# Two seven-product units of a decoder layer: the second unit's first weight sum, its row-sum fetches and the gate fetches are issued at other places

## The chip, the cores and the metric

The kernel is one program on one NeuronCore of a Trainium2 chip. TensorE (PE in the profile) multiplies, VectorE (DVE), ScalarE (ACT) and GpSimd (POOL) do the element-wise work, SyncE (SP) and GpSimd issue the DMAs that matter here. The metric is the device time of one execution in microseconds; lower is better. Three executions of the kernel before gave 883.59, 883.69 and 885.77 us, median 883.69.

## The reference, cut to what matters

One decoder layer on 512 tokens of width 1024, float32: a LayerNorm, then a token mixer in which gated linear attention (GLA, 4 heads) and latent attention run on the same input, then a squared-ReLU MLP. The part that concerns this change is the input projection of GLA's value `v_g` and gate `r_g`, both 512x1024 by 1024x1024, and what is done with them:

```python
q_g, k_g, v_g, r_g, a_lr, q_lat, kv_lat, gate_logits = jnp.split(h @ w_in, offsets, axis=-1)
o_gla = gla_chunked(split_heads(q_g) * GLA_HK ** -0.5, split_heads(k_g), split_heads(v_g), split_heads(log_a))
o_gla = rms_norm(o_gla.transpose(0, 2, 1, 3), gla_norm_g.reshape(GLA_HEADS, GLA_HV))
y_gla = (o_gla * jax.nn.silu(r_g)) @ w_o_gla
```

## The kernel before, in words

**Precision.** Every float32 operand is split in a high part (a rounding copy by ACT, L185 or L111) and a low part (a subtraction by DVE, L186 or L112). A product then is three matmuls: high x high, high x low, low x high. A weight item is a 128 x 1024 tile of 4 KB a partition, and its split is one ACT and one DVE instruction.

**The two units.** `unit("r")` and later `unit("v")` compute the two 512x1024 by 1024x1024 projections with seven block products in place of eight. A unit has seven phases, n = 0 to 6, each of two halves (hf = 0, 1) of 12 matmuls (L755 to L757), so 24 matmuls of 512 columns a phase. The phases multiply the weight operands `RPH = ("T1", "11", "22", "T2", "21", "T3", "T4")`. "11" and "21" are plain weight blocks, loaded by SP as `wraw` (L173). "22" is a plain block loaded by POOL as `rw`. The T's are sums of blocks that the DMA makes: `r_begin` loads a block into two `rw` tiles (T1) and then adds a second block into the same tiles with an accumulating DMA (L614); later `r_add` turns T1 into T2, T2 into T4 and "22" into T3 by further accumulating DMAs into the same tile, each of which has to wait until the split has read the former sum.

**The row sums.** The other operand of phases 0, 2, 3 and 5 is a sum of blocks of the input rows, called S1, S4, S2 and S3. They are made once while `unit("r")` is near, split, used by it and stored to DRAM (`keep`, L631). For `unit("v")` they are fetched again by POOL (`fetch`, L636): two tiles of 512 KB each.

**Order of the work.** The program is traced in one order; `tick` after each half phase advances other lanes of work (the GLA levels of each head, the SiLU of the gates, `gla_out`). A planner then orders every engine's instructions: it runs through the program with its own estimated durations and gives an engine, among the instructions whose inputs and tile slots it takes to be ready, the one that was traced first. On the chip every engine executes its list strictly in that order.

**Slots.** Tiles of 4 KB a partition (`rw`, the fetched row sums `S`, the gate and value results `rg`, the split pairs xh/xl, `qk`, `kq`, `sd` and others) share 24 slots, tag "A". Tiles of 2 KB share 22 slots, pool "B". The high and low weight tiles `whi` and `wlo` have two slots each; items take either these ("w") or a pair xh/xl from the 24 ("a"), in the order `wawawawawawaww`, so the last two items of a unit (T4) and the first of the next (T1, half 0) go through whi/wlo.

**The gates and `gla_out`.** `silus()` turns the four results of `unit("r")` into SiLU and stores them (`rd`, L728). `gla_out(h)`, one of four heads, runs after `unit("v")`. It fetches the head's gates from DRAM on SP's queue (L930, two DMAs of 256 KB into one 4 KB tile `rg`), computes four output tiles i = 0 to 3, normalises, multiplies with the gates (L971), and transposes (L978).

Of the kernel before, what the change touches and what calls it, by code (L numbers as in the profile page):

```python
# [10 lines left out]
F32 = mybir.dt.float32  # L11
# [41 lines left out]
def tile_hybrid_block(ctx: ExitStack, tc: tile.TileContext, I, out, dbg=None):  # L53
# [19 lines left out]
    def A(shape, dt=F32, n="a"):  # L73
        tag, bufs = ("C", 8) if n in TAG_C else (n, TAG_W[n]) if n in TAG_W else ("A", 24)
        return pa.tile(shape, dt, tag=tag, bufs=bufs, name=nm(n))
# [540 lines left out]
    def r_begin(sec):  # L616
        for hf in range(2):
            r_load(sec, "T1", 0, 1, hf)
        r_add(sec, "T1", "T1", 0, 0)
# [13 lines left out]
    def fetch(name):  # L633
        RS[name] = [A([P, 4, 256], F32R, name) for _ in range(2)]
        for d, w in zip(KEPT[name], RS[name]):
            nc.gpsimd.dma_start(w, d)  # L636
# [63 lines left out]
    def unit(sec, nxt=None):  # L700
        a, b = [[MM() for _ in range(2)] for _ in range(2)]
        R = {}
        val = sec == "v"

        def put(key, t, o, scale=1.0):
            if key not in R:
                R[key] = A([P, 2, T], F32, "rg")
            r = R[key][:, t]
            act(r, o, AF.Copy, scale=scale)

        def last(key, t, o, op):
            r = R[key][:, t]
            vtt(r, r, o, op=op)
            if val:
                if t == 0:
                    R["v" + key] = [A([P, 2, T], F32R, n) for n in ("vh", "vl")]
                split(r, *[w[:, t] for w in R["v" + key]])

        def silus():
            for key in ("12", "11", "22", "21"):  # L720
                for t in range(2):
                    r = R[key][:, t]
                    th = B([P, T], F32, "th")
                    act(th, r, AF.Tanh, scale=0.5)
                    stt(r, th, 1.0, r, op0=ALU.add, op1=ALU.mult)
                    yield
                d = DR([P, 2, T], F32, "rd")
                nc.sync.dma_start(d, R[key])  # L728
                R[key] = d
                yield  # L730
            Rp[0], Rp[1] = [R["11"], R["21"]], [R["12"], R["22"]]

        def lhs(n, k, t):
            c = slice(t * P, (t + 1) * P)
            d = slice(256 + t * P, 256 + (t + 1) * P)
            if n in (1, 4):
                h = hT[k + 4 * (n == 4)]
                return h[:, 0, c], h[:, 1, c]
            if n == 6:
                return hT[k + 4][:, 0, d], hT[k + 4][:, 1, d]  # L740
            key = {0: "S1", 2: "S4", 3: "S2", 5: "S3"}[n]
            while not val and key not in RS:
                step(t_rs)
            return [w[:, k, c] for w in RS[key]]

        for n in range(7):
            o = a if n in (1, 3, 5) else b
            for hf in range(2):
                pump(PL[sec, n, hf])
                for pp in range(2):  # L750
                    for t in range(2):
                        xh, xl = lhs(n, 2 * hf + pp, t)
                        hi, lo = [w[:, pp] for w in stream[PL[sec, n, hf]]["w"]]
                        opens = n in (0, 1, 4, 6) and hf == 0 and pp == 0
                        mm(o[t], xh, hi, start=opens, stop=False, skip_group_check=True)  # L755
                        mm(o[t], xh, lo, start=False, stop=False, skip_group_check=True)
                        mm(o[t], xl, hi, start=False, stop=hf == 1 and pp == 1, skip_group_check=True)  # L757
                if hf == 0 and (val or n in (0, 2, 4, 6)):
                    tick(None)
                if n == 0 and hf == 1:  # L760
                    r_add(sec, "T2", "T1", 1, 1)
                    if val:
                        fetch("S2")
                if n == 2 and hf == 1:
                    r_add(sec, "T3", "22", 0, 1)
                    if val:
                        fetch("S3")
                if n == 3 and hf == 1:
                    r_add(sec, "T4", "T2", 1, 0)
                if n == 5 and hf == 0 and nxt:  # L770
                    r_begin(nxt)
                    fetch("S1")
                    fetch("S4")
                if n == 6 and hf == 0 and nxt:
                    for h2 in range(2):
                        r_load(nxt, "22", 1, 1, h2)
            for t in range(2):
                if n == 0:
                    put("22", t, o[t], -1.0)
                elif n == 1:  # L780
                    put("11", t, o[t])
                elif n == 2:
                    put("12", t, o[t], -1.0)
                elif n == 3:
                    last("12", t, o[t], ALU.subtract)
                elif n == 4:
                    last("11", t, o[t], ALU.add)
                elif n == 5:
                    put("21", t, o[t])
                    last("22", t, o[t], ALU.subtract)  # L790
                else:
                    last("21", t, o[t], ALU.add)
            if n < 6:
                tick(None)
        if val:
            for j in range(2):
                Vp[j] = [R["v%d%d" % (i, j + 1)] for i in (1, 2)]
        else:
            t_sil.append(spawn(silus()))
# [124 lines left out]
    def gla_out(h):  # L924
        while SS[h] is None or Vp[h // 2] is None or Rp[h // 2] is None:
            yield
        sd, s128, kq = SS[h]
        rg = A([P, NT, HV], F32, "rg")
        for i in range(2):
            nc.sync.dma_start(rg[:, 2 * i:2 * i + 2], Rp[h // 2][i][:, :, h % 2 * HV:(h % 2 + 1) * HV])  # L930

        def V(j):
            c = slice(h % 2 * HV, (h % 2 + 1) * HV)
            return [t[:, j % 2, c] for t in Vp[h // 2][j // 2]]
        p = PX()[:, :HV]
        for j in range(2):
            vh, vl = V(j)
            kh, kl = [kq[:, 0, w, j * P:(j + 1) * P] for w in range(2)]
            mm(p, kh, vh, start=j == 0, stop=False)
            mm(p, kh, vl, start=False, stop=False)  # L940
            mm(p, kl, vh, start=False, stop=j == 1)
        sh, sl = B([P, HV], F32R, "gst"), B([P, HV], F32R, "gst")
        split(p, sh, sl)
        ss = S([P, NT], F32, "gss")
        ps = []
        for i in range(NT):
            if i % 2 == 0:
                ps.append(PX())
            o = ps[i // 2][:, (i % 2) * HV:(i % 2 + 1) * HV]
            todo = [(sd[:, 0, i, :], sd[:, 1, i, :], *V(i))]  # L950
            if i % 2:
                todo.append((s128[:, 0, i // 2, :], s128[:, 1, i // 2, :], *V(i - 1)))
            if i > 1:
                c = slice((i - 2) * P, (i - 1) * P)
                todo.append((kq[:, 1, 0, c], kq[:, 1, 1, c], sh, sl))
            for n, (ah, al, bh, bl) in enumerate(todo):
                mm(o, ah, bh, start=n == 0, stop=False)
                mm(o, ah, bl, start=False, stop=False)
                mm(o, al, bh, start=False, stop=n == len(todo) - 1)
            sq = B([P, HV], F32, "osq")  # L960
            act(sq, o, AF.Square, accum_out=ss[:, i:i + 1])
            if i >= 1:
                yield
        vts(ss, ss, 4.0 / HV, 4.0 * RMS_EPS, op0=ALU.mult, op1=ALU.add)
        rs = S([P, NT], F32, "grs")
        gtt(rs, ss, mhalf[:, :NT], op=ALU.pow)
        yield
        og = [B([P, 2, HV], F32, "og") for _ in range(2)]
        for i in range(NT):
            o = ps[i // 2][:, (i % 2) * HV:(i % 2 + 1) * HV]  # L970
            stt(og[i // 2][:, i % 2, :], o, rs[:, i:i + 1], rg[:, i],  # L971
                op0=ALU.mult, op1=ALU.mult)
        yield
        for kk in range(2):
            k = 2 * h + kk
            p = PX()
            for tt in range(NT):
                nc.tensor.transpose(p[:, tt * P:(tt + 1) * P], og[tt // 2][:, tt % 2, kk * P:(kk + 1) * P], ident)  # L978
            yield
            o = A([P, 2, T], F32R, "ogT")  # L980
            split(p, o[:, 0, :], o[:, 1, :], scale=glg[:, k:k + 1])
            ogT[k] = o
# [574 lines left out]
```

## Time and profile before

| | |
|---|---|
| median of three executions | 883.69 us |
| the profiled execution, device time | 883.45 us |
| its span, first to last instruction | 881.7 us |
| PE busy | 854.5 us, 97% of the span |
| DVE, ACT, POOL busy | 610.0, 466.2, 188.0 us |
| mean granted TensorE clock | 0.994 |

The profile was taken on one execution. Its times count from the first instruction, so 1.75 us of the device time lie outside the span. "Idle before" is the time an engine did nothing ahead of an instruction, with the event that ended it. `unit("r")` runs from 94.9 to 139.1 us, `unit("v")` from 145.5 to 193.0 us, and the four heads of `gla_out` from 192.8 to 307 us.

### The profile page before, as it was taken

The page shows a single profiled execution, that of the slowest core. Times are in us where ns is not written, and L with a number is a line of the kernel's source. Part 1 is how long each engine was busy: PE and PEld are TensorE (multiplying, and loading weights), DVE is VectorE, ACT ScalarE, POOL GpSimd, SP SyncE. Part 2 cuts the span into 40 slices and gives each one's busy share as a digit, 9 for nine tenths or more (in the row PEclk, how much of TensorE's full clock was granted, in tenths as well). Part 3 has the DMA queues.
Part 4 walks back from the last instruction along what each step waited for, and adds up shares of the span by engine and source line. Part 5 has one row for each costly group of instructions (what it writes and reads, how often), then busy time and mean ns, then how long its engine had stood idle before and what let it go on. Part 6 is the DMA issues. An engine that isn't in the chain of part 4 may idle for free. (4 is left out here: it accounts for less than half of the span.)

```text
span 881.7 us, 11628 instructions
## 1 busy us (share of the span) xinstructions
PE 854.5 (97%) x4288; PEld 726.2 (82%) x4288; DVE 610.0 (69%) x993; ACT 466.2 (53%) x802; POOL 188.0 (21%) x221
## 2 busy tenths in 40 slices
PE   5999997999999999999999999999999999999995
PEld 5988785778898888888988888988888888888885
DVE  7977986796556344557876797886567556754697
ACT  5467765564554433435654414565457546735662
POOL 2404683603202010000000013004400520242023
PEclk9999998999999999999999999999999999999998
DMA  7836898933454223111307527006941990398075
GB/s 229 241 103 218 250 267 227 250 124 105 122 176 120 63 63 105 52 53 55 109 25 261 191 76 282 1 1 168 291 114 30 260 256 27 68 304 202 0 191 96
DMA packets 73240, 127.35 MB, mean 144 GB/s; under 512 B 8641, under 2 KB 34676, under 8 KB 73184
## 3 DMA queue, kind: packets, MB, share of 16 engines
q1 hardware_dynamic: 50848, 70.86, 24.8%
q0 software_dynamic: 20416, 52.11, 24.7%
q10 hardware_dynamic: 1920, 3.66, 1.2%
q8 instruction: 33, 0.54, 0.2%
q14 instruction: 23, 0.19, 0.1%
HBM read 99.86 MB, written 12.58 MB: 128 GB/s over the span
## 5 line engine op out<-in xcount | busy, mean ns | idle before, releaser
L186 DVE TENSOR_TENSOR wlo<-wraw,whi 128x1024 fp32r<-128x1024 f32 (+2 forms) x90 | 102.2, 1137 | 97.8 <-ACT whi L185 92.0
L236 PE MATMUL mm<-h,whi 128*128 128x512 f32 x416 | 163.2, 393 | 0.1
L237 PE MATMUL mm<-h,whi 128*128 128x512 f32 x416 | 162.8, 391 | 0.0
L238 PE MATMUL mm<-h,wlo 128*128 128x512 f32 x416 | 155.9, 391 | 0.1
L185 ACT ACTIVATE whi<-wraw 128x1024 fp32r<-128x1024 f32 (+2 forms) x90 | 87.0, 967 | 69.9 <-PE mm L237 34.5
L1419 POOL DMA_DIRECT2D res<-ev x54 | 47.8, 992 | 237.6 <-ACT ev L1417 194.2
L236 PEld LDWEIGHTS mm<-h,whi 128*128 128x128 f32 x416 | 78.2, 188 | 16.0 <-ACT whi L185 0.3
L238 PEld LDWEIGHTS mm<-h,wlo 128*128 128x128 f32 x416 | 77.9, 188 | 16.2 <-DVE wlo L186 0.5
L237 PEld LDWEIGHTS mm<-h,whi 128*128 128x128 f32 x416 | 78.2, 188 | 15.1
L1484 ACT ACTIVATE relu<-mm 128x512 f32<-128x512 f32 x32 | 18.8, 595 | 56.9 <-PE mm L238 56.9
L374 POOL TENSOR_TENSOR mv<-mv,mhalf 128x1 f32<-128x1 f32 x4 | 4.1, 1036 | 208.5 <-DVE mv L373 208.5
L185 ACT ACTIVATE xh<-wraw 128x1024 fp32r<-128x1024 f32 (+1 forms) x24 | 23.2, 974 | 26.8 <-PE mm L271 15.4
L614 POOL DMA_DIRECT2D rw<-in_w_in_dram x24 | 26.1, 1128 | 32.6 <-DVE xl L186 12.9
L186 DVE TENSOR_TENSOR wlo<-wq,whi 128x1024 fp32r<-128x1024 f32 x15 | 18.4, 1224 | 19.9 <-ACT whi L185 19.9
L856 ACT ACTIVATE M<-qk 128x256 f32<-128x256 f32 x56 | 23.9, 454 | 14.1 <-DVE qk L838 13.3
L186 DVE TENSOR_TENSOR xl<-wraw,xh 128x1024 fp32r<-128x1024 f32 (+1 forms) x24 | 27.0, 1137 | 6.3 <-ACT xh L185 6.3
L1417 ACT ACTIVATE ev<-mm 128x512 f32<-128x512 f32 x20 | 11.9, 600 | 31.6 <-DMA res<-ev 27.8
L838 DVE TENSOR_TENSOR qk<-qk,tot 128x512 f32<-128x512 f32 x28 | 23.5, 840 | 7.1 <-PE px L894 4.2
L1334 POOL DMA_DIRECT2D wq<-in_w_ff_dram x32 | 24.5, 1024 | 11.1 <-issue 4.6
L236 PE MATMUL mm<-ogT,whi 128*128 128x512 f32 x64 | 25.7, 401 | 0.0
L237 PE MATMUL mm<-ogT,whi 128*128 128x512 f32 x64 | 25.3, 395 | 0.0
L237 PE MATMUL mm<-omT,whi 128*128 128x512 f32 x64 | 25.2, 394 | 0.0
(457 smaller groups left out, 2413.6 us busy)
## 6 DMA issues: line engine op xcount, KB each, us to landing
wraw<-in_w_in_dram SPq DMA_DIRECT2D x32, 512.0 KB, 4.6
wraw<-in_w_ff_dram SPq DMA_DIRECT2D x32, 512.0 KB, 8.6
wq<-in_w_ff_dram POOLq DMA_DIRECT2D x32, 512.0 KB, 9.9
res<-ev POOLq DMA_DIRECT2D x54, 256.0 KB, 8.6
rw<-in_w_in_dram POOLq DMA_DIRECT2D x24, 512.0 KB, 7.7
S<-s SPq DMA_DIRECT2D x8, 512.0 KB, 6.4
S<-S POOLq DMA_DIRECT2D x8, 512.0 KB, 7.1
wraw<-in_w_o_gla_dram SPq DMA_DIRECT2D x8, 512.0 KB, 3.7
```

The source lines that it names most:

```text
L185: st["ins"] = act(hi[:, :nk, :n], raw[:, :nk, :n], AF.Copy)
L186: vtt(lo[:, :nk, :n], raw[:, :nk, :n], f(hi[:, :nk, :n]), op=ALU.subtract)
L236: mm(o, hi[:, c], xh, start=first, stop=False)
L237: mm(o, hi[:, c], xl, start=False, stop=False)
L238: mm(o, lo[:, c], xh, start=False, stop=last)
L614: nc.gpsimd.dma_start(RW[sec, op, hf], w[:, k0:k0 + 2, c0:c0 + T], **({"accum_op": ALU.add} if add else {}))
L838: vtt(new, new, view(tot, o + 1, -1, 2, 0, s), op=ALU.mult)
L856: act(packed(M, s, i), half_lr(qk, s, i), AF.Copy)
L1334: nc.gpsimd.dma_start(t, w2[:, k0:k0 + 3:2, j * T:(j + 1) * T])
L1417: st["ev"] = act(e, o, AF.Copy, scale=-1.0 if ph == 4 else 1.0)
L1419: nc.gpsimd.dma_start(res[tt + t][:, j * T:(j + 1) * T], e, accum_op=ALU.add)
L1484: act(r, ps, AF.Relu)
```

## The change

Four edits.

1. `unit("r")`: `r_begin("v")` (two loads and two accumulating loads of T1) is traced at phase 3, half 0, in place of phase 5, half 0.
2. The fetch of S1 for `unit("v")` is traced at phase 5, half 1 of `unit("r")`, in place of half 0.
3. The fetch of S4 moves from phase 5, half 0 of `unit("r")` to phase 0, half 0 of `unit("v")`.
4. `gla_out`: the head's gates are fetched after the third output tile in place of at the start, into two tiles of 2 KB of pool "B" in place of one of 4 KB of the 24 slots.

```diff
@@ unit @@
-                if n == 5 and hf == 0 and nxt:
+                if n == 3 and hf == 0 and nxt:
                     r_begin(nxt)
+                if n == 5 and hf == 1 and nxt:
                     fetch("S1")
+                if n == 0 and hf == 0 and val:
                     fetch("S4")
                 if n == 6 and hf == 0 and nxt:
@@ gla_out @@
-        rg = A([P, NT, HV], F32, "rg")
-        for i in range(2):
-            nc.sync.dma_start(rg[:, 2 * i:2 * i + 2], Rp[h // 2][i][:, :, h % 2 * HV:(h % 2 + 1) * HV])
...
             act(sq, o, AF.Square, accum_out=ss[:, i:i + 1])
+            if i == 2:
+                rg = []
+                for j in range(2):
+                    rg.append(B([P, 2, HV], F32, "rgb"))
+                    nc.sync.dma_start(rg[j], Rp[h // 2][j][:, :, h % 2 * HV:(h % 2 + 1) * HV])
...
-            stt(og[i // 2][:, i % 2, :], o, rs[:, i:i + 1], rg[:, i],
+            stt(og[i // 2][:, i % 2, :], o, rs[:, i:i + 1], rg[i // 2][:, i % 2],
                 op0=ALU.mult, op1=ALU.mult)
```

Nothing of the arithmetic changes, and the number and sizes of the DMAs stay as they were.

## The prediction

> **What bounds the kernel now.** I read the shares of the page first, then the waits of PE, then the timeline around PE's longest wait, then the clock by stretches, then the DMA issues that this wait hangs on.
>
> The page's shares say that PE is the bound, so only PE's own idle time and slow time can be won:
>
> ```profile
> span 881.7 us, 11628 instructions
> PE 854.5 (97%) x4288; PEld 726.2 (82%) x4288; DVE 610.0 (69%) x993; ACT 466.2 (53%) x802; POOL 188.0 (21%) x221
> ```
>
> The waits of PE name where its idle time is:
>
> ```profile
> PE mm L755 <- ACT whi L185: 5.1, 1, 5.1
> PE mm L756 <- DVE wlo L186: 2.2, 2, 1.9
> ```
>
> The first, one wait of 5.1 us, stands between the two seven-product units; the second line's two are in the second unit. The timeline around it:
>
> ```profile
> 124.94 1.50 POOL L614 DMA_DIRECT2D rw<-in_w_in_dram  x2
> 126.44 2.18 POOL L636 DMA_DIRECT2D S<-S  x4
> 129.77 4.07 POOL L614 DMA_DIRECT2D rw<-in_w_in_dram  x4 [1.15 <-DMA rw<-in_w_in_dram]
> 133.34 0.48 PE L755 MATMUL mm<-whi,h 128*128 128x512 f32 x1
> 139.78 0.61 PE L891 MATMUL px<-M 128*128 128x128 f32 x4
> 143.44 1.06 ACT L185 ACTIVATE xh<-rw 128x1024 fp32r<-128x1024 f32 x1 [6.98 <-DMA rw<-in_w_in_dram]
> 145.49 1.22 PE L755 MATMUL mm<-whi,S 128*128 128x512 f32 x2 [5.11 <-ACT whi L185]
> 145.67 1.22 DVE L186 TENSOR_TENSOR wlo<-rw,whi 128x1024 fp32r<-128x1024 f32 x1
> 146.94 0.79 PE L756 MATMUL mm<-wlo,S 128*128 128x512 f32 x1 [0.23 <-DVE wlo L186]
> ```
>
> Read it from the end. PE has nothing from 140.39 to 145.49, then starts the second unit. It waited for the split of T1, and ACT had waited 6.98 us for a landing. That landing is T1's second accumulating DMA. POOL issued T1's loads at 124.94, then the four row-sum fetches, then the accumulating DMAs from 129.77. So the first weight sum of the second unit arrives too late, behind two megabytes of row sums.
>
> The same stretch costs more than its idle time, as the table by stretches shows (PEclk, the granted clock, is the third number from the end of a row):
>
> ```profile
> 140.40:143.40 3.00, 0.00 (x0) 0.00 (x0) 0.00 (x0) 0.00 (x0) 0.00 (x0) 1.00 1.05 370
> 143.40:150.20 6.80, 4.48 (x10) 3.09 (x11) 5.67 (x7) 5.93 (x10) 4.36 (x5) 0.50 0.34 90
> 171.90:177.10 5.20, 3.25 (x16) 2.50 (x16) 5.20 (x6) 2.33 (x6) 4.84 (x6) 1.00 1.04 239
> ```
>
> The clock was granted at 0.50 from 143.4 to 150.2, and PE was at work for 150.20 - 145.49 = 4.71 us of that.
>
> **The change part by part.**
>
> *The stall that goes.* Idle 5.11 + 0.23 = 5.34 us, and half of the 4.71 us at half clock, 2.36 us: together 7.70 us. The Trainium skill, page "TensorE: Matmul & The Clock Gate", part 1, says that one idle window of about 3.4 us halves the clock, and a busy one of as much brings it back. By that rule the second term would be an estimate of 3.4 / 2 = 1.7 and the sum 7.0 us; the trace's 4.71 us are the longer stretch, and I go by them. The last row agrees in kind: it holds the other unit stall, 1.95 us, and the clock stayed at 1.00.
>
> *T1 two phases sooner (four POOL DMAs).* The rows of these and of r's own T4 sums, which POOL issues at 111.67 and 117.88 and which are now traced behind them; then ACT's splits of T4:
>
> ```profile
> 111.67 1.20 POOL L614 DMA_DIRECT2D rw<-in_w_in_dram  x1 [0.83 <-DVE wlo L186]
> 117.88 1.21 POOL L614 DMA_DIRECT2D rw<-in_w_in_dram  x1 [1.78 <-DVE xl L186]
> ...
> 125.57 1.05 ACT L185 ACTIVATE whi<-rw 128x1024 fp32r<-128x1024 f32 x1
> 130.96 1.06 ACT L185 ACTIVATE whi<-rw 128x1024 fp32r<-128x1024 f32 x1 [3.74 <-issue]
> ```
>
> Issue to landing, from the DMA view of single issues, in the order T1's first load (124.94), its first and second accumulation (129.77, 131.11), r's two T4 sums (111.67, 117.88):
>
> ```profile
> rw<-in_w_in_dram POOLq DMA_DIRECT2D x1, 512.0 KB, 4.3
> ...
> rw<-in_w_in_dram POOLq DMA_DIRECT2D x1, 512.0 KB, 9.7
> ...
> rw<-in_w_in_dram POOLq DMA_DIRECT2D x1, 512.0 KB, 12.3
> ...
> rw<-in_w_in_dram POOLq DMA_DIRECT2D x1, 512.0 KB, 9.9
> ...
> rw<-in_w_in_dram POOLq DMA_DIRECT2D x1, 512.0 KB, 6.5
> ```
>
> The planner can put the loads between 111 and 119 us, around the T4 sums. At the latest: loads at 119.1, landed 4.3 later, accumulations as slow as now (12.3): landed at 135.7. The deadline is set by whi. T1's half 0 needs a whi slot that T4's half 0 holds until the 12 matmuls of phase 6, half 0 are through, near 136.1 (the phase's 24 matmuls begin at 133.34, and small matmuls of the head lane follow them until 139.78 + 0.61 = 140.39). Then 1.05 on ACT and 1.22 on DVE: ready near 138.5. PE is covered until 140.39 by the second half phase and those small matmuls, so no idle is left. If the cover were short, PE would wait for the remainder; I take 0, ends 0 and 1.5.
>
> What this costs r: T4's sums land at 111.67 + 9.9 = 121.6 and 117.88 + 6.5 = 124.4, and are split at 125.57 and 130.96, so 4.0 and 6.6 us of slack. Two loads ahead of them take 2 x 0.524 MB / 370 GB/s = 2.8 us of transfer (rate of the first row by stretches): covered. Were the accumulations ahead as well, T4 would come up to 12.3 us later, 133.9, and with 2.3 us of splitting PE would wait some 2.9 us at phase 6. I take 0: accumulations wait for their loads, so the planner has the T4 sums ready first. Two of the 24 slots are held longer: by the code I count 18 or 19 live at phase 3, so they fit.
>
> *S1 half a phase later (two POOL DMAs).* Now issued at 126.44. Half a phase is 2.7 us, and T1's accumulations may be ahead: issue at 130 to 133, and the landing row
>
> ```profile
> S<-S POOLq DMA_DIRECT2D x4, 512.0 KB, 7.2
> ```
>
> gives 137 to 140, against 140.39. Two fetches fewer stand in this queue. I take 0; the upper end is the 1.5 above.
>
> *S4 into the second unit (two POOL DMAs).* It leaves the queue ahead of T1 and enters it ahead of T2, the next sum, which is on the edge today:
>
> ```profile
> 162.49 1.06 ACT L185 ACTIVATE whi<-rw 128x1024 fp32r<-128x1024 f32 x1 [6.23 <-DMA rw<-in_w_in_dram]
> 163.58 1.23 DVE L186 TENSOR_TENSOR wlo<-rw,whi 128x1024 fp32r<-128x1024 f32 x1 [5.92 <-ACT whi L185]
> 165.28 0.48 PE L755 MATMUL mm<-whi,S 128*128 128x512 f32 x1
> ...
> 148.19 1.61 POOL L636 DMA_DIRECT2D S<-S  x2
> 149.29 1.75 POOL L614 DMA_DIRECT2D rw<-in_w_in_dram  x1
> ...
> rw<-in_w_in_dram POOLq DMA_DIRECT2D x1, 512.0 KB, 13.1
> ```
>
> T2's half 0 was issued at 149.29 and landed 13.1 later; PE took it at 165.28, 0.5 us after DVE was done. From the end of T1's DVE split (146.9) to T2's (164.8) are 17.9 us. In the changed kernel T1's split ends near 138.5, so T2 is ready at 156.4. PE, starting at 140.39, reaches phase 3 after 165.28 - 145.49 - 0.23 - 2.36 = 17.2 us, at 157.6. The two S4 fetches in front add up to 2.8 us: ready at 159.2, a stall of 1.6. But S2's two fetches, which stood before T2's half 0 (148.19), may now stand behind: then none. I take 1.0 us, ends 0 and 3.0. S4 itself, issued from 139 on and landing 7.2 later, is there before phase 2 (near 152).
>
> *The other stall of the second unit.* DVE's split took 2.77 us in place of 1.22, while POOL worked, and PE waited 1.95:
>
> ```profile
> 171.47 2.77 DVE L186 TENSOR_TENSOR wlo<-wraw,whi 128x1024 fp32r<-128x1024 f32 x1
> 172.67 3.78 POOL L813 TENSOR_TENSOR tot<-tot 128x64 f32<-128x64 f32 x4
> 174.30 0.50 PE L756 MATMUL mm<-wlo,h 128*128 128x512 f32 x1 [1.95 <-DVE wlo L186]
> ```
>
> Nothing of the change removes it, but the order around it is planned anew: 0, ends -1.95 and +1.95.
>
> *The gates in two 2 KB tiles.* Eight SP DMAs before and after, moved within `gla_out`:
>
> ```profile
> DMA to landing us min/median/max: 3.7/4.5/5.9
> ...
> 202.40 0.43 ACT L961 ACTIVATE osq<-px 128x256 f32<-128x256 f32 x1
> ...
> L971 DVE SCALAR_TENSOR_TENSOR og<-px,grs,rg x16: 469/474/485, 213.8 to 302.4; 128x256 f32<-128x256 f32 x16
> ```
>
> For head 0 the third tile's square sum is at 202.40 and the first use at 213.8, 11.4 us apart against a landing of at most 5.9. SP may hold a weight transfer in front that waits for its buffer; then the gates come later, and PE, which has gate projections to do, would wait only at the transposes. One of the 24 slots is freed for some 10 us a head, two of the 22 taken. I take 0, ends -0.5 and +2.
>
> **Sum.** 881.7 - 7.7 + 1.0 = 875.0 us of span, with the 1.75 us outside it 876.75. The profiled execution (883.45) is 0.24 under the median, so 877.0 us.
>
> **The rivals.** Within 0.3% (2.65 us) a change can't be told from none here.
>
> *DVE and the next sums take part of it back.* With 7.7 us less, the second unit asks DMA and DVE for the same work in less time. For: T2's slack of 0.5 us, and DVE's slow split. Price: T2's 3.0 and a doubled DVE stall of 1.95 in place of my 1.0, so 877.0 + 2.0 + 1.95 = 881. The Trainium skill, page "SBUF — State Buffer", section "SBUF: two separate sides", says why: a DVE operation with two SBUF inputs and a GpSimd operation exclude each other for a whole instruction; the 2.77 us beside POOL's work agree.
>
> *It doesn't do what it says.* The planner has no two slots at phase 3, and T1's loads go out where they do now. Then only S4's absence helps, by 2.8 us plus the half clock (2.36), and T2 (3.0) and DVE (1.95) take it back: 883.5.
>
> *Slower: S4 is fetched into a full pool.* S4's slots may come only from r's stored gates. The first store was issued at 136.64, the second at 157.09 and landed 8.5 later:
>
> ```profile
> 157.09 0.34 SPq L728 DMA_DIRECT2D rd<-rg  x1
> ...
> rd<-rg SPq DMA_DIRECT2D x1, 512.0 KB, 8.5
> ```
>
> Shifted by 7.7 that is 157.9; S4 lands 7.2 later, at 165, and PE, at phase 2 near 152, waits 13 us and loses 2.36 more to the clock: 877.0 - 1.0 + 15.4 = 891. It ends on the slow side once S4 lands after about 160. Against it: in the trace S2 got two slots at 148.2 while S4 was still live.
>
> **How the numbers follow.** The forecast, stall gone, 874 to 879: 0.55. Part taken back, 879 to 883: 0.20 (0.17 of it faster). No effect: 0.07. Slower: 0.18. That makes faster 0.72, same 0.10, slower 0.18. The range takes the forecast with the DVE stall gone as well (883.7 - 7.7 - 1.95 = 874.0, a little under for unknowns) to the end of the second case: 873.5 to 883.0.
>
> **What would show it.** Right: no PE wait over 1 us on T1's split between the units, PEclk 1.00 there, T1's accumulations landed before 136, S4 before phase 2. Wrong: a PE wait on a row sum, on T2 or T4, a clock of 0.50 anywhere in the units, or idle PE in `gla_out`.

## The result, and the profile after

The changed kernel took 872.54 us (median of four, 872.33 to 873.04). The kernel before, beside it on the same chip, took 883.64. The ratio is 0.987, its 95% interval 0.9853 to 0.9887, so the gain is 11.1 us. The prediction said 877.0 us, 873.5 to 883.0. Its direction held, and the time lies just below its range.

The page's first lines of the changed kernel, and then the one wait of PE that is left at the lines of the two units (us in total, times, longest):

```profile
span 870.8 us, 11623 instructions
PE 850.5 (98%) x4288; PEld 724.9 (83%) x4288; DVE 607.2 (70%) x993; ACT 466.6 (54%) x802; POOL 181.5 (21%) x221
```

```profile
PE mm L755 <- ACT s L111: 0.6, 1, 0.6
```

The waits of 5.1 and 1.9 us are gone; the wait on `s` stands at the start of `unit("r")`, as before. PE's other waits lie in the first 20 us and at 544 us, outside the units. The timeline of the changed kernel around the place of the first one and of T2 (start, duration, engine, line):

```profile
116.17 1.51 POOL L614 DMA_DIRECT2D rw<-in_w_in_dram  x2
124.24 2.52 POOL L614 DMA_DIRECT2D rw<-in_w_in_dram  x2 [0.82 <-DMA rw<-in_w_in_dram]
134.16 1.12 POOL L636 DMA_DIRECT2D S<-S  x2 [2.56 <-PE mm L757]
136.71 1.06 ACT L185 ACTIVATE xh<-rw 128x1024 fp32r<-128x1024 f32 x1
138.11 1.07 ACT L185 ACTIVATE whi<-rw 128x1024 fp32r<-128x1024 f32 x1
140.72 0.61 PE L893 MATMUL px<-M 128*128 128x128 f32 x4
141.08 0.71 PE L755 MATMUL mm<-whi,S 128*128 128x512 f32 x2
142.41 1.28 POOL L614 DMA_DIRECT2D rw<-in_w_in_dram  x1
154.53 1.06 ACT L185 ACTIVATE whi<-rw 128x1024 fp32r<-128x1024 f32 x1 [0.46 <-DMA rw<-in_w_in_dram]
155.62 1.22 DVE L186 TENSOR_TENSOR wlo<-rw,whi 128x1024 fp32r<-128x1024 f32 x1 [0.49 <-ACT whi L185]
158.77 3.16 DVE L186 TENSOR_TENSOR wlo<-wraw,whi 128x1024 fp32r<-128x1024 f32 x1
158.77 0.71 PE L755 MATMUL mm<-whi,S 128*128 128x512 f32 x2
```

T1's loads go out at 116.17 and its accumulations from 124.24; S4's fetch comes at 134.16. T1's splits (136.71, 138.11) wait for no landing, and PE goes from the head lane's matmuls at 140.72 straight into the second unit at 141.08. T2's half 0 (issued 142.41) is split from 154.53 and done at 156.84; PE takes it at 158.77, so its slack is 1.9 us where it was 0.5. The next row is DVE's split of "21", on which PE had its second wait: beside POOL it is still slow (3.16 us), but it ends at 161.9, before phase 4, which PE begins at 164.79.

The clock column of the changed kernel stays at 1.00 in the stretch that was at 0.50 before:

```profile
140.40:143.40 3.00, 3.00 (x17) 2.56 (x16) 3.00 (x5) 2.72 (x7) 3.00 (x5) 1.00 1.10 328
143.40:150.20 6.80, 6.80 (x33) 5.70 (x33) 6.80 (x11) 4.23 (x7) 1.80 (x3) 1.00 1.11 314
```

**The balance.** The profiled executions are 883.45 and 872.6 us, 10.85 apart. For every matmul between 130 and 320 us I took the time from its start to the next one's start, less what that form of matmul usually takes. The sum is 13.2 us in the kernel before and 1.2 in the changed one. Of the 13.2, 7.9 lie at the first gap and the half clock behind it, 2.3 at the second gap, and the rest is small pieces of 0.1 to 0.3 us; these fell from 3.0 to 1.2. That makes 12.0. The changed kernel's `unit("r")` began 0.96 us later (95.83 against 94.87, the first L755), in a part the change doesn't touch, which leaves 11.0. (That part scatters: over the profiles of this document the unit begins between 94.87 and 96.16.)

### The profile page after: what moved, and what is told of

Its sections match the earlier page's. It is cut to its first block, busy times and chain, and to the rows that moved or that the text cites. A ratio compares the mean times of both kernels' runs of the same rounds, so it can differ in the third digit from the quotient of the medians.

```text
span 870.8 us, 11623 instructions
## 1 busy us (share of the span) xinstructions
PE 850.5 (98%) x4288; PEld 724.9 (83%) x4288; DVE 607.2 (70%) x993; ACT 466.6 (54%) x802; POOL 181.5 (21%) x221
## 5 line engine op out<-in xcount | busy, mean ns | idle before, releaser
L840 DVE TENSOR_TENSOR qk<-qk,tot 128x512 f32<-128x512 f32 x28 | 20.9, 746 | 7.6 <-ACT M L858 3.8
```

The lines of the kernel that those rows point to most:

```text
L840: vtt(new, new, view(tot, o + 1, -1, 2, 0, s), op=ALU.mult)
```

## The experiments

Two theories stood at the start. A: the late T1 is the head of one chain; the half clock, T2's lateness and the second wait all follow from it. B: the second wait is a loss of its own, from DVE's split meeting POOL's work, and each loss has to be taken away separately.

### The edits apart

The first edit alone: T1 begun at phase 3, both fetches left where they were.

```diff
-                if n == 5 and hf == 0 and nxt:
+                if n == 3 and hf == 0 and nxt:
                     r_begin(nxt)
+                if n == 5 and hf == 0 and nxt:
                     fetch("S1")
                     fetch("S4")
```

> The kernel before with T1's load and accumulation traced at phase 3, half 0; S1 and S4 are fetched at phase 5, half 0 as before, the gates as before. Theory A (one late chain): T1's lateness makes the 5.34 us of idle PE and 2.36 us of half clock, and, by T2's late landing, also the 1.95 us wait in the second unit and about 1 us of small slips; this edit alone brings nearly all of the 11.1 us: 872 to 874.5, both waits gone. Theory B (separate stalls): the 1.95 us are DVE held up by POOL and go for another reason; this edit brings 7.7 us: 875.5 to 877, and a PE wait of 1 to 2 us on wlo stays in the second unit.

Measured: 875.3 us (875.0 to 875.93), ratio 0.9901 [0.9885, 0.9918]. The time lies between the two forecasts. The first wait and the half clock (the stretch at 0.50) are gone, and of the second wait 0.4 us is left, though nothing was done about it. Its row among the waits of PE, and ACT's split of T2's half 0:

```profile
PE mm L756 <- DVE wlo L186: 0.4, 1, 0.4
```

```profile
153.90 1.06 ACT L185 ACTIVATE whi<-rw 128x1024 fp32r<-128x1024 f32 x1 [4.44 <-DMA rw<-in_w_in_dram]
```

Edits 2 and 3 alone: S1 half a phase later, S4 in the second unit, T1 as before.

```diff
                 if n == 5 and hf == 0 and nxt:
                     r_begin(nxt)
+                if n == 5 and hf == 1 and nxt:
                     fetch("S1")
+                if n == 0 and hf == 0 and val:
                     fetch("S4")
```

> The kernel before with S1's fetch at phase 5, half 1 and S4's at phase 0, half 0 of the second unit; T1 stays at phase 5, half 0. Theory A: two transfers of some 1.4 us leave the queue ahead of T1's accumulations, so T1 lands 2 to 4 us sooner; the wait of 5.1 us shrinks to 1 to 3 us, too short for the half clock: 876 to 880. Theory B: the same first stall, but the 1.95 us wait stays: 878.5 to 881. If the accumulations don't move up, 883 to 884.

Measured: 878.69 us (875.49 to 879.14), ratio 0.9929 [0.991, 0.9948]. T1's second half lands at 139.9 in place of 143.4, and ACT waits for it 3.83 us in place of 6.98. PE then loses 1.4 us on ACT's next work and 0.8 on the split, and nothing at the second place. The profiled execution is the 875.49 one and shows no half clock. The other three are about 3 us longer, at a mean granted clock of 0.992 where the profiled one has 0.997, so they spent more time at half clock; they were not profiled, and what brought it on is open.

```profile
139.93 1.06 ACT L185 ACTIVATE xh<-rw 128x1024 fp32r<-128x1024 f32 x1 [3.83 <-DMA rw<-in_w_in_dram]
141.60 0.71 PE L893 MATMUL px<-M 128*128 128x128 f32 x4 [1.44 <-ACT M L858]
144.03 0.50 PE L756 MATMUL mm<-wlo,S 128*128 128x512 f32 x1 [0.85 <-DVE wlo L186]
```

The gates alone, edit 4 on the kernel before:

```diff
-        rg = A([P, NT, HV], F32, "rg")
...
+            if i == 2:
+                rg = []
+                for j in range(2):
+                    rg.append(B([P, 2, HV], F32, "rgb"))
...
```

> The kernel before with the gates fetched after the third output tile into two 2 KB tiles, and nothing else. Theory A: no effect beyond noise, 882.5 to 884.5, the waits of 5.1 and 1.95 us as before. Rival C (the gates hold a slot or SP's queue): at least 1 us of the gain comes from here, 880 to 882.5.

Measured: 883.67 us, ratio 0.9996 [0.9987, 1.0006]: no difference.

Edits 1 to 3 without the gates:

```diff
+                if n == 3 and hf == 0 and nxt:
                     r_begin(nxt)
+                if n == 5 and hf == 1 and nxt:
                     fetch("S1")
+                if n == 0 and hf == 0 and val:
                     fetch("S4")
```

> The changed kernel with the gates as before (edits 1 to 3). Theory A: 872 to 873.3, as the changed kernel. Rival C: 873.5 or more.

Measured: 872.98 us (872.71 to 873.37), ratio 0.9873 [0.9858, 0.9888], the changed kernel's time. So edit 4 is worth nothing, as forecast. Edit 1 alone gives 8.8 us, edits 2 and 3 alone 5.4, and together they give 11.1, not 14.2: in large part they mend the same thing.

### Is the second wait a loss of its own?

The kernel before, with S2's fetch moved from in front of T2's half 0 to behind it:

```diff
                     r_add(sec, "T2", "T1", 1, 1)
-                    if val:
-                        fetch("S2")
+                if n == 1 and hf == 1 and val:
+                    fetch("S2")
```

> The kernel before with one edit: S2's fetch for the second unit is traced at phase 1, half 1, so that it stands behind both of T2's accumulations in POOL's queue. T1 stays late. Theory A (the 1.95 us wait comes from T2's late landing, which holds up ACT's in-order list): T2's half 0 lands 2 to 4 us sooner after its issue than 13.1, the first wait stays at about 5 us, the second falls under 0.6 us: 881 to 882.7. Theory B (DVE slowed by POOL is enough): the second wait stays at 1.5 to 2.5 us: 883.5 to 885. S2 behind T2 may itself be late for phase 3: then a new wait of up to 3 us on S there, 884 to 887.

Measured: 880.04 us (879.94 to 881.43), ratio 0.9953 [0.9936, 0.9969]. The timeline:

```profile
145.80 1.02 PE L755 MATMUL mm<-whi,S 128*128 128x512 f32 x2 [4.54 <-ACT whi L185]
147.25 0.79 PE L756 MATMUL mm<-wlo,S 128*128 128x512 f32 x1 [0.43 <-DVE wlo L186]
158.80 1.06 ACT L185 ACTIVATE whi<-rw 128x1024 fp32r<-128x1024 f32 x1 [2.69 <-DMA rw<-in_w_in_dram]
167.76 2.79 DVE L186 TENSOR_TENSOR wlo<-wraw,whi 128x1024 fp32r<-128x1024 f32 x1
```

The first wait stays (4.54 us, and 0.43 on the low half behind it). ACT stands only 2.69 us ahead of T2's split, where it stood 6.23, and the second wait of 1.95 us is gone: DVE's split of "21" ends at 170.55, and PE takes it at 171.80. DVE's split beside POOL takes 2.79 us here too. So the slow split is not enough to make the wait; B falls in that form. The time lies 1 us below theory A's range. Behind the first wait the clock was at half for 3.41 us here, for 6.83 in the kernel before, and by the steps of PE that place cost 1.0 us less.

The changed kernel with S4 fetched in the first unit again, both fetches at phase 5, half 1:

```diff
                 if n == 5 and hf == 1 and nxt:
                     fetch("S1")
-                if n == 0 and hf == 0 and val:
                     fetch("S4")
```

> The changed kernel with S4 fetched together with S1 at phase 5, half 1 of the first unit. T1 is early in both. If T1's place is what counts, 872 to 873.5 and no wait over 0.5 us. If S4's deferral counts by itself (transfers ahead of '22' and T2 are late), 873.5 to 876 with a wait of 0.3 to 1.5 us on a weight split in the second unit.

Measured: 875.62 us (875.22 to 876.08), ratio 0.9898 [0.9883, 0.9913]. The second wait is back in full, with T1 in time and no half clock:

```profile
155.05 1.06 ACT L185 ACTIVATE whi<-rw 128x1024 fp32r<-128x1024 f32 x1 [6.19 <-PE mm L757]
160.56 1.04 ACT L185 ACTIVATE whi<-wraw 128x1024 fp32r<-128x1024 f32 x1
164.03 2.77 DVE L186 TENSOR_TENSOR wlo<-wraw,whi 128x1024 fp32r<-128x1024 f32 x1
166.85 0.50 PE L756 MATMUL mm<-wlo,h 128*128 128x512 f32 x1 [1.95 <-DVE wlo L186]
```

So A falls too as it stood: the second wait is not merely the first one's follow-on. And T2 is hardly later here: half 0's split starts at 155.05, against 154.53 in the changed kernel (1.0 us later, counted from the unit's start). (The row names a matmul as the releaser, but T2's sum landed only at 154.97.) What differs is ACT's list. Here ACT comes to this split after 148.9 and stands in front of it for 6.19 us, with the copies of phase 1's results and the next splits queued behind; in the changed kernel these come first, and ACT stands 0.46 us. "21" is then split from 160.56 in place of 157.15.

ACT's wait ahead of T2's half 0, against PE's wait on the split of "21", over the runs so far:

| kernel | ACT stood, us | PE's second wait, us |
|---|---|---|
| before | 6.23 | 1.95 |
| gates alone | 5.92 | 1.86 |
| S4 in the first unit | 6.19 | 1.95 |
| T1 alone | 4.44 | 0.41 |
| S2 behind T2 | 2.69 | 0 |
| changed kernel | 0.46 | 0 |

Edits 2 and 3 alone, edits 1 to 3, and the runs below except the last have 0 to 0.7 us of ACT there and no wait of PE; the last has 6.33 and 1.02.

### The order of ACT's list

This was met first in a run meant for B. In the kernel before, the totals and products of the head lane (POOL's L813 to L824) are traced later, so that DVE's splits meet less of POOL's work; no fetch is moved:

```diff
-            if s == 16 and h + 1 < GH:
+            if s == 64 and h + 1 < GH:
```

> The kernel before with the next head's totals and products (POOL's work beside the split of '21') traced at level 64 in place of 16. T1 and T2 stay late. Theory A alone: the second wait is lateness and stays at 1.5 to 2.5 us, 883.5 to 885. Theory B: without POOL beside it DVE's split takes 1.2 us in place of 2.77, and of the 1.95 us wait at most 0.5 us is left, 881 to 883. Both together (lateness brings the split to the edge, POOL's work makes the wait): 0.3 to 0.6 us are left, 881.5 to 883.

Measured: 874.61 us (873.83 to 875.01), ratio 0.9885 [0.987, 0.99]. This is 6 us below the lowest forecast. Both waits are gone, although T1's accumulations go out no sooner (129.93 against 129.77) and its second half lands at 142.3 (before: 143.4):

```profile
129.93 2.48 POOL L614 DMA_DIRECT2D rw<-in_w_in_dram  x2
138.40 1.06 ACT L185 ACTIVATE whi<-rw 128x1024 fp32r<-128x1024 f32 x1
142.32 1.06 ACT L185 ACTIVATE xh<-rw 128x1024 fp32r<-128x1024 f32 x1 [2.34 <-DMA rw<-in_w_in_dram]
141.89 0.71 PE L755 MATMUL mm<-whi,S 128*128 128x512 f32 x2
```

Here ACT splits half 0 (`whi`) first, at 138.40, and half 1 (`xh`) when it lands. The kernel before does it the other way round: half 1 at 143.44, after 6.98 us, and half 0 at 144.40, which had landed at 129.77 + 9.7 = 139.5. The row of half 0 in the kernel before, which follows the one with the 6.98 us:

```profile
144.40 1.04 ACT L185 ACTIVATE whi<-rw 128x1024 fp32r<-128x1024 f32 x1
```

PE needed half 0 first. So theory A was put anew: a late landing costs PE little by itself; what costs is the work that stands behind the waiting split in ACT's list.

The test: in the kernel before, half 1's split may not stand ahead of half 0's. No DMA is moved.

```diff
-                for g in st["gates"]:
+                for g in (*st["gates"], *([st["ins"]] if st["spl"] == PL.get(("v", 0, 1)) else [])):
```

> The kernel before with one order fixed: ACT's split of half 1 of the second unit's T1 may not stand ahead of the split of half 0. No DMA is moved. In the kernel before half 0 of T1 had landed at 139.45, but ACT split half 1 first and waited for it until 143.42. Theory A (the first stall is T1's landing time plus ACT's list order, and the second stall follows from the first): half 0 is split from 139.5 to 140.6 on ACT and to 141.8 on DVE, PE waits 0.1 and then about 1.2 us; half 1, landed at 143.4, is split until 145.7, when PE is through half 0 at about 144.5, so another wait of up to 1.2 us; together 1.3 to 2.5 in place of 5.3, no time at half clock, 877 to 880 us; if the second stall goes with it, 875 to 878. Rival (the landing alone sets the stall, the order does not matter): the wait moves to half 1 with its full length, 4 us or more in all, clock at 0.50 again, 882 to 885.

Measured: 876.57 us (876.33 to 876.86), ratio 0.9907 [0.9892, 0.9922]. No half clock; its timeline:

```profile
140.65 1.06 ACT L185 ACTIVATE whi<-rw 128x1024 fp32r<-128x1024 f32 x1 [3.10 <-PE px L913]
141.75 0.73 PE L755 MATMUL mm<-whi,S 128*128 128x512 f32 x2 [0.28 <-ACT whi L185]
143.01 0.50 PE L756 MATMUL mm<-wlo,S 128*128 128x512 f32 x1 [0.53 <-DVE wlo L186]
144.18 1.06 ACT L185 ACTIVATE xh<-rw 128x1024 fp32r<-128x1024 f32 x1 [2.48 <-DMA rw<-in_w_in_dram]
146.55 0.50 PE L756 MATMUL mm<-xl,S 128*128 128x512 f32 x1 [0.52 <-DVE xl L186]
151.31 0.50 PE L756 MATMUL mm<-wlo,h 128*128 128x512 f32 x1 [1.28 <-DVE wlo L186]
```

T1's half 1 lands as late as ever (144.2), and PE waits 0.28 + 0.53 + 0.52 = 1.3 us in place of 5.3, with another 1.28 in phase 1. At the second place it waits no more, as theory A's second figure (875 to 878) has it. With the two instructions of ACT turned round the kernel is 8 us faster: the order, not the landing alone, made the first wait. By the steps of PE, about 4 of the 8 us lie at the first place and 2 at the second. The planner made all lists anew, so more than these two instructions moved; POOL's totals of the head lane, for one, begin at 162.28 in place of 165.86. The loss at the second place goes with the new lists as a whole; this run doesn't say which part of them took it away.

The same test at the second place: S4 in the first unit, as in the run with the 6.19 us, and T2's split kept behind the copies of phase 1's results (`put` stores its ACT instruction).

```diff
-                for g in st["gates"]:
+                for g in (*st["gates"], *([st["put"]] if st["spl"] == PL.get(("v", 3, 0)) else [])):
...
-            act(r, o, AF.Copy, scale=scale)
+            st["put"] = act(r, o, AF.Copy, scale=scale)
```

> The kernel of the run with S1 and S4 both fetched in the first unit, with one order fixed: ACT's split of T2, half 0, may not stand ahead of the copies of phase 1's results. There, ACT stood for 6.2 us ahead of this split, whose sum landed at 155.0, and the split of 21 came 5 us later than in the changed kernel, although T2 landed at nearly the same time (154.5 there). No DMA is moved. Theory A, as it now stands (a late landing costs little by itself; what costs is the ACT work queued behind the waiting split): ACT's wait ahead of T2's split falls below 1.5 us, the DVE split of 21 starts 3 us or more sooner, the 1.95 us wait of PE goes, 872.3 to 874.0 us. Theory B (the 1.95 us come from DVE and POOL meeting, and T2's landing has to be sooner): the wait stays at 1.5 us or more, 875 to 876.5.

Measured: 872.06 us (871.55 to 872.44), ratio 0.9862 [0.9846, 0.9879], the lowest time of all, though not to be told from the changed kernel's (0.987). ACT and DVE in the timeline:

```profile
152.93 0.59 ACT L709 ACTIVATE rg<-mm 128x512 f32<-128x512 f32 x1
153.41 1.07 ACT L185 ACTIVATE whi<-rw 128x1024 fp32r<-128x1024 f32 x1
156.03 1.05 ACT L185 ACTIVATE whi<-wraw 128x1024 fp32r<-128x1024 f32 x1
157.46 1.22 DVE L186 TENSOR_TENSOR wlo<-wraw,whi 128x1024 fp32r<-128x1024 f32 x1
```

ACT comes to T2's split at 153.41, when the sum has just landed (153.39), and no work is held up behind it. The split of "21" begins at 157.46 in place of 164.03, 6.6 us sooner; 1.6 of them are T2's landing, which came at 154.97 there. PE has no wait in the unit. DVE's split takes 1.22 us here; POOL's work fell beside the next one, which took 3.19. By itself this run does not settle the matter: T2's sooner landing and the fast split would have ended the split at 164.03 - 1.6 + 1.22 = 163.7, before PE came to it at 164.9. The changed kernel does: there T2 landed only 0.5 us sooner than with S4 in the first unit and the split was slow (3.16 us), and it still began 5.3 us sooner. So what moving S4 won came, for the larger part, from the order of ACT's list that the planner made of it; with that order forced, S4 can stay in the first unit.

### How soon must T1 be?

The changed kernel with `r_begin` one phase later, which is one phase sooner than in the kernel before:

```diff
-                if n == 3 and hf == 0 and nxt:
+                if n == 4 and hf == 0 and nxt:
                     r_begin(nxt)
```

> The changed kernel with T1 traced at phase 4, half 0, one phase later, so that POOL issues its loads after the T4 sums and an accumulation stands behind S1. How much of the lead is needed: T1's last accumulation should land near 139 to 141; the first matmul of the second unit waits 0 to 2 us, no half clock, 872.5 to 875. If every microsecond of lateness counts twice (a wait, then the half clock), 877 to 880.

Measured: 872.69 us (872.2 to 874.14), ratio 0.9867 [0.9853, 0.9882]. The sums land at 133.6 and 137.9; PE waits 0.5 us. One phase sooner would have done.

And half a phase later still:

```diff
-                if n == 3 and hf == 0 and nxt:
+                if n == 4 and hf == 1 and nxt:
                     r_begin(nxt)
```

> The changed kernel with T1's loads and sums begun at phase 4, half 1, of the first unit in place of phase 3, half 0: half a phase ahead of where the kernel before begins them. With the beginning at phase 4, half 0, the sums landed at 133.6 and 137.9, and the time was that of the changed kernel. Half a phase is 2.7 us: landings near 136.3 and 140.6. Theory A (the stall is a step: nothing until the landing passes the time at which PE is through the first unit, 141, less 2.3 us of splitting): half 0 just in time, half 1 at 143 needed at 144: no wait over 1.5 us, 872.3 to 874.5. Rival (each 2.7 us of T1's start cost as much, in steps down to the kernel before's 5.3 us): a wait of 2 to 3 us, 875 to 878.

Measured: 875.74 us (875.33 to 878.24), ratio 0.9903 [0.9884, 0.9923]: the rival's time. Half 1 lands at 140.5, ACT again stands for it first (4.12 us), with half 0 landed (137.6) and its split behind, and what PE waits for first is another piece of ACT's work:

```profile
140.52 1.06 ACT L185 ACTIVATE xh<-rw 128x1024 fp32r<-128x1024 f32 x1 [4.12 <-DMA rw<-in_w_in_dram]
...
142.19 0.71 PE L893 MATMUL px<-M 128*128 128x128 f32 x4 [1.73 <-ACT M L858]
```

### Both together

The changed kernel with the totals traced at 64 as well:

```diff
-            if s == 16 and h + 1 < GH:
+            if s == 64 and h + 1 < GH:
```

> The changed kernel with the level totals traced at level size 64 in place of 16, which by itself took 9 to 10 us off the kernel before. Theory A (both take away the same late chain): nothing is left to gain, 871.5 to 873.5 us, and no PE wait over 1.5 us between 130 and 200 us. Rival (they take away different losses): 866 to 870 us.

Measured: 879.79 us (879.22 to 880.84), ratio 0.9946 [0.9928, 0.9964]: 7 us slower than the changed kernel, and above both forecasts. The timeline:

```profile
142.03 0.73 PE L755 MATMUL mm<-whi,S 128*128 128x512 f32 x2 [1.18 <-ACT whi L185]
144.79 0.54 POOL L636 DMA_DIRECT2D S<-S  x1 [1.79 <-DMA rd<-rg]
145.32 1.26 POOL L614 DMA_DIRECT2D rw<-in_w_in_dram  x1
158.42 1.06 ACT L185 ACTIVATE whi<-rw 128x1024 fp32r<-128x1024 f32 x1 [6.33 <-DMA rw<-in_w_in_dram]
169.82 0.50 PE L756 MATMUL mm<-wlo,h 128*128 128x512 f32 x1 [1.02 <-DVE wlo L186]
```

POOL waits 1.79 us for the store of a gate tile ahead of S2's second fetch, and T2's half 0 stands behind it: issued at 145.32 in place of 142.41. ACT stands 6.33 us ahead of its split. PE's steps between 130 and 330 us are 8.7 us longer than usual, against 1.2. Two edits that each take out the stall make new lists in which waits of PE on splits are back, at both places, though no half clock in the units. The gains don't add.

## Why the prediction was right or wrong

**The stall that goes: right, and sized well.** 7.70 us forecast; 7.9 by the steps of PE. By the figure of the Trainium skill, "TensorE: Matmul & The Clock Gate", part 1, the prediction's other estimate was 7.0, with one window of 3.4 us of slow clock; the kernel before had two (below).

**What made it: half right.** The prediction read the 6.98 us of ACT as the landing of T1 behind the row sums, and stopped there. It did not ask which half PE needed. Half 0 had landed 4 us before, and ACT's list held its split behind half 1's. The rows quoted there showed it: the one that waits is `xh`, PE's is `whi`. The forecast of the change came out the same, because with T1 landed early the order doesn't matter.

**T1 two phases sooner, S1 later, the gates: right.** All at 0, and the runs show none of them costing anything. Gates alone measured 0.9996. T4 was not made late.

**S4 into the second unit, +1.0: the step that failed, with the next.** The forecast let S4's two fetches delay T2 by their 2.8 us of transfer: 17.9 + 2.8 = 20.7 us from the end of T1's DVE split to T2's. It was 16.1 (140.77 to 156.84). S4 was traced at phase 0 of the second unit, but POOL issued its two fetches at 134.16 and 134.71, ahead of T2's half 1 (139.33), S2 and T2's half 0 (142.41). They landed at 141.5 and 143.9, one before T2's half 0 was issued and one 1.5 us after. T2's half 0 landed 12.1 us after its issue (13.1 before) and had 1.9 us of slack. The term was 0. More than that, with S4 in the first unit the ratio is 0.9898 in place of 0.987, some 2.5 us, for the larger part by ACT's order: the edit was charged 1.0 us and was worth 2.5.

**The other stall, 0: failed.** "Nothing of the change removes it" took the cause from the instruction next to the wait, DVE's split beside POOL. That split is still slow (3.16 us, where 1.22 is usual; the Trainium skill's "SBUF — State Buffer", section "SBUF: two separate sides", fits that), yet it costs nothing when it starts in time. The start was set by ACT, 6.23 us idle ahead of T2's split; that row was quoted too, for T2 alone. 1.95 us of idle time, 2.3 by the steps.

**Not in the sum.** Small steps of 0.1 to 0.3 us behind the stalls, 1.8 us in all; and the start, 0.96 us the other way. So: 6.7 forecast, + 0.2 at the stall, + 1.0 for T2, + 2.3 for the second wait, + 1.8, - 0.96 = 11.0, measured 10.85. The lower end of the range was set at 874.0, with S4 at 0 and the other stall gone, and "a little under for unknowns". The sum had no term for the small steps, and they are what lies below it: 874.0 - 0.2 - 0.35 - 1.8 + 0.96 = 872.6.

**The rivals.** "Take part of it back" (881), "doesn't do what it says" (883.5) and "a full pool" (891) did not happen. The last one's mechanism, a fetch that waits for a stored gate, shows in the last experiment, at S2 and with 1.79 us.

## What to carry to other kernels

When an engine stands in front of one instruction until a DMA lands, read what stands behind it in its list and which of it the bottleneck needs first: here, turning two instructions round (and planning the rest anew) was worth 8.2 us, and moving T1's DMAs alone 8.8. A wait on a slow instruction is a question about when that instruction started, so follow the chain back until an engine stood idle, before a stall is called independent of the change. Where a planner makes the lists, an edit's gain is the gain of the new lists, and gains of two edits can't be added.

## What the runs showed of the hardware

The granted clock keeps to windows of 3.413 us, which is also its shortest stretch at 0.50 on record (in the gates alone and in S2 behind T2): in the records of the kernel before it was at 1.00, 0.50 and 1.00 for 129.7, 6.83 and 727.0 us, which are 38, 2 and 213 such windows. And a window need not be idle throughout to bring the half clock. Tables by such windows (us, then busy time of PE, PEld, DVE, ACT, POOL, then the granted clock, the DMA share and GB/s). The kernel before, at its second wait:

```profile
170.71:174.12 3.41, 1.64 (x10) 1.17 (x8) 3.41 (x2) 2.84 (x6) 3.41 (x4) 1.00 0.96 205
174.12:177.54 3.42, 3.24 (x16) 2.81 (x17) 3.42 (x7) 1.11 (x3) 2.62 (x5) 1.00 1.07 326
```

and the kernel with the gates alone, at the same wait:

```profile
171.94:175.35 3.41, 1.55 (x9) 1.16 (x8) 3.41 (x4) 2.18 (x4) 3.25 (x5) 1.00 0.92 160
175.35:178.77 3.42, 3.42 (x10) 2.65 (x9) 3.42 (x5) 1.78 (x5) 2.11 (x3) 0.50 1.09 371
```

PE was busy for 1.64 us of the window, 48%, and the clock stayed; 1.55 us, 45%, and it fell to 0.50 for the next window. A wait of 1.9 us was enough. At the first wait the kernel before has two windows under that, and two at half clock behind them; S2 behind T2 has one such window (0.27 us) and one at half clock. The kernel before:

```profile
139.99:143.40 3.41, 0.40 (x4) 0.20 (x2) 0.00 (x0) 0.00 (x0) 0.00 (x0) 1.00 1.06 360
143.40:146.82 3.42, 1.22 (x2) 0.50 (x2) 2.29 (x3) 3.38 (x5) 0.98 (x1) 0.50 0.39 156
146.82:150.23 3.41, 3.29 (x8) 2.62 (x9) 3.41 (x6) 2.54 (x6) 3.41 (x5) 0.50 0.28 25
```

The Trainium skill, "TensorE: Matmul & The Clock Gate", part 1, has the free-running window of about 3.4 us, and these runs agree; that less than half of it busy suffices is from these rows, which hold two points and no more. Getting the full clock back is another matter: with the gates alone PE was busy for 1.74 us, 51%, of the half-clock window from 144.62 to 148.04, and the next window was at half clock too. What a wait near 2 us costs then depends on where the window's edge falls in it, so the same program may or may not pay the half clock. The executions of the kernel before have mean granted clocks from 0.992 to 0.995.
